# Attention on one core: seven product units in each bank, and q and k rounded to fp16 by GpSimd's loading queue from the second batch on

## The chip, the cores and the metric

The kernel runs on one core of a Trainium2 chip. The metric is the device time of one execution in microseconds; lower is better. Most executions of a kernel agree within a per cent. The "granted clock" below is the share of its full clock that TensorE was given, as the profile records it. The span that a profile gives is shorter than the time by about 1.8 us, in the kernel before.

## The reference

It is plain softmax attention: 8 batches of 8 heads, 512 positions, 64 dimensions, all fp32.

```python
def reference(q, k, v):                       # each (8, 8, 512, 64) fp32
    scale = 1.0 / np.sqrt(q.shape[-1])
    scores = np.einsum('bhqd,bhkd->bhqk', q, k) * scale
    scores = scores - scores.max(axis=-1, keepdims=True)
    attn = np.exp(scores)
    attn = attn / attn.sum(axis=-1, keepdims=True)
    return np.einsum('bhqk,bhkd->bhqd', attn, v).astype(np.float32)
```

## The kernel before

The 64 heads are handled as 32 pairs. For each pair, q, k and v come in as fp32 from the SyncE queue, 256 KB each, and GpSimd rounds them to fp16. For q and k it also lays the two heads side by side, so that one transpose of 128 columns serves both.

```python
def load(g, names):                            # one pair: 128 x (2 heads x 4 x 64) fp32
    ...
        nc.sync.dma_start(out=t[:, :, :, :], in_=source(src, g))

def cast_qk(g):
    t = qpool.tile([P, 2, NI, P], FP16, tag="qkp", name=f"qkp_{g}")
    for n, name in ((1, "k"), (0, "q")):
        nc.gpsimd.tensor_copy(
            out=t[:, n].rearrange("p i (h d) -> p h i d", h=2),
            in_=raw[g][name][:, :, :, :],
        )

def transposes(g, n):                          # n = 0: q, n = 1: k; tps is one PSUM bank
    ...
    for i in range(NI):
        nc.tensor.transpose(tps[g][:, n, i, :], qkp[g][:, n, i, :], ident)
```

VectorE copies the bank of a pair's transposes out. Scores are matmuls of 64x512; two of them make a group of 128x1024, which ScalarE turns into exponentials (`pt`). Products of `pt` with v (and a column of ones) fill one bank for each head: four units of 65 columns. VectorE divides by the sum and stores.

```python
def normalise(g, h):
    o = os.pop((g, h))                         # 128 x 4 x 65
    nc.vector.reciprocal(out=rc[:, :, :], in_=o[:, :, D : D + 1])
    nc.vector.tensor_tensor(out=ob[:, h], in0=o[:, :, 0:D],
                            in1=rc[:, :, :].broadcast_to([P, NI, D]), op=AluOp.mult)
    if g == LAST:
        nc.sync.dma_start(out=source(out, g)[:, h], in_=ob[:, h])
    elif not first:                            # the pair's second head
        nc.sync.dma_start(out=source(out, g), in_=ob[:, :, :, :])
```

Four of the 129 groups are given to VectorE instead of ScalarE: a "raise" and ten passes of integer and polynomial work. A small planner in Python (`Plan`), with estimated durations, fixes the order of all instructions when the kernel is built. Each engine then works through its list in order, so an instruction that isn't ready holds all that stand behind it on its engine.

The softmax here doesn't subtract the row's maximum and nothing guards it: scores larger than these inputs give would overflow.

Of the kernel before, what the change touches and what calls it, by code (L numbers as in the profile page):

```python
# [14 lines left out]

class Plan:

# [7 lines left out]
    T_UNIT, V_UNIT = 224, 130  # L25
    TO_ACT, TO_DVE, TO_PE = 275, 210, 60
    COPY, NORM = 700, 640
    RAISE, PASS, LATE = 1210, 690, 300
    STEP = 5

    def __init__(self, groups, pairs, first, share):
        self.groups, self.pairs, self.share = groups, pairs, share
        self.pe, self.act, self.dve = 6700, 7820, 6800
        self.m, self.tiled = first, True
        self.done = {}
        self.exps = {}
        for m in range(first):
            self.done[m] = self.exps[m] = 6000 + m * 904 + self.EXP_DONE
        self.tq = {0: 6800}
        self.next_t = 1  # L40
        self.bank = [6000, 6800]
        self.jobs = 0
        self.job = None
        self.todo = [(g, h) for g in range(pairs) for h in range(2)]
        self.member = {}
        for m, grp in enumerate(groups):
            for b in grp:
                self.member[b] = m
        self.evacs = []
        self.raises = []  # L50
        self.poly = []
        self.steps = []

# [9 lines left out]
    def blocks_done(self, g, h, chunks=range(4)):  # L63
        return max(self.exps.get(self.member[(g, c, h)], 1e9) for c in chunks)

    def free(self, m):
        g = self.groups[m][0][0]
        return max(self.done.get(m - 3, 1e9) if m >= 3 else 0, self.tq.get(g, 1e9))

    def issue(self, t):  # L70
        m, grp = self.m, self.groups[self.m]
        g = grp[0][0]
        heads = [b[2] for b in grp]
        slots = 1 if len(set(heads)) == 2 else len(grp)
        on_dve = (
            self.share
            and not self.poly
            and not self.raises
            and 2 <= g < self.pairs - 7
            and m % 4 == 1  # L80
        )
        self.note(t, "scores", m, on_dve)
        t += (0 if self.tiled else self.INTO) + self.SLOT * slots
        self.tiled = True
        if on_dve:
            self.raises.append((t + self.TO_DVE, m))
        else:
            n = len(grp)
            begin = max(self.act, t + self.TO_ACT)
            self.act = begin + self.EXP * n // 2 + self.EXP_FIXED  # L90
            self.done[m] = self.exps[m] = self.act + self.EXP_DONE - self.EXP - self.EXP_FIXED
        self.m += 1
        self.pe = t

    def pick(self, t):
        cur = self.groups[min(self.m, len(self.groups) - 1)][0][0]
        n = self.jobs
        if t + 40 < self.bank[n % 2]:
            return None
        g = self.next_t  # L100
        can_t = g < self.pairs and g <= cur + 2 and t >= self.ready_kq(g)
        if can_t and g <= cur + 1:
            return ("t", g)
        for g2, h in self.todo[:8]:
            last = (g2, h) == (self.pairs - 1, 1)
            chunks = (0,) if last else range(4)
            if t >= self.blocks_done(g2, h, chunks) and t >= self.ready_v(g2):
                return ("v", g2, h)
        return ("t", g) if can_t else None

    def unit_ready(self):
        what, part = self.job[0], self.job[1]
        if what[0] == "v" and what[1:] == (self.pairs - 1, 1):
            return self.blocks_done(what[1], what[2], (part,))
        return 0

    def fill(self, t):
        if self.job is None:
            what = self.pick(t)
            if what is None:  # L120
                return False
            self.job = [what, 0, self.jobs]
            self.jobs += 1
            self.bank[self.job[2] % 2] = 1e9
            if what[0] == "t":
                self.next_t += 1
            else:
                self.todo.remove(what[1:])
        if t < self.unit_ready():
            return False  # L130
        what, part, n = self.job
        cost = (self.T_UNIT if what[0] == "t" else self.V_UNIT) + (self.OUT_OF if self.tiled else 0)
        self.tiled = False
        self.note(t, "unit", what, part)
        self.pe = t + cost
        self.job[1] += 1
        if self.job[1] == (2 if what[0] == "t" else 4):
            self.evacs.append((self.pe + self.TO_DVE, what, n))
            self.job = None
        return True  # L140

    def step_pe(self, t):
        if self.m < len(self.groups):
            now = t >= self.free(self.m)
            more = self.m + 1 < len(self.groups) and t >= self.free(self.m + 1)
            slack = self.act - t
            if now and (more or slack < 1100):
                return self.issue(t)
            soon = self.free(self.m)
            if not now and slack < 1300 and soon < t + 150:  # L150
                return
        else:
            now = False
        if not self.fill(t) and now:
            self.issue(t)

    def step_dve(self, t):
        if self.raises and self.raises[0][0] <= t:
            ready, m = self.raises.pop(0)
            self.note(t, "raise", m)  # L160
            self.dve = t + self.RAISE
            self.done[m] = self.dve + self.TO_PE
            self.poly = [(m, s) for s in range(10)]
            return
        if self.evacs and self.evacs[0][0] <= t:
            ready, what, n = self.evacs.pop(0)
            self.note(t, "evac", what)
            self.dve = t + (self.COPY if what[0] == "t" else self.NORM)
            self.bank[n % 2] = self.dve + self.TO_PE
            if what[0] == "t":  # L170
                self.tq[what[1]] = self.dve + self.TO_PE
            return
        coming = [x[0] for x in self.raises + self.evacs]
        if self.poly and min(coming, default=1e9) > t + self.PASS - self.LATE:
            m, s = self.poly.pop(0)
            self.note(t, "pass", m, s)
            self.dve = t + self.PASS
            if s == 9:
                self.exps[m] = self.dve + self.TO_PE

    def run(self):
        t = min(self.pe, self.dve)
        while self.m < len(self.groups) or self.todo or self.job or self.evacs or self.poly:
# [8 lines left out]

# [3 lines left out]
def kernel(  # L196
# [27 lines left out]
    M = len(groups)  # L224
# [3 lines left out]
    qpool = ctx.enter_context(tc.tile_pool(name="qk16", bufs=3))  # L228
    tpool = ctx.enter_context(tc.tile_pool(name="tqk", bufs=4))
    ppool = ctx.enter_context(tc.tile_pool(name="pt", bufs=36))  # L230
# [6 lines left out]
    NV = 12  # L237
    vps = [cpool.tile([P, 2, NI, D + 1], FP16, name=f"vp{n}") for n in range(NV)]
# [9 lines left out]
    obs = {}  # L248
# [6 lines left out]
    def load_tile(g, name):  # L255
        t = lpool.tile([P, 2, NI, D], FP32, tag=f"{name}32", name=f"{name}32_{g}")
# [10 lines left out]

    def cast_v(g):
        nc.gpsimd.tensor_copy(out=vps[g % NV][:, :, :, 0:D], in_=raw[g]["v"][:, :, :, :])  # L269

    def cast_qk(g):
        if g >= NP:
            return
# [7 lines left out]

    def transposes(g, n):
# [3 lines left out]
        for i in range(NI):  # L286
            nc.tensor.transpose(tps[g][:, n, i, :], qkp[g][:, n, i, :], ident)  # L287
# [6 lines left out]
    def scores(m, on_dve=False):  # L294
# [41 lines left out]
    def pass_(m, s):  # L336
# [12 lines left out]
        if s == 1:  # L349
# [10 lines left out]
        n, x = divmod(s - 2, 2)  # L360
        mant = r["m"][:, x, :].bitcast(FP32)
        nc.vector.scalar_tensor_tensor(  # L362
            out=r["pt"][:, x, :] if n == 3 else r["y"][:, x, :],
            in0=mant if n == 0 else r["y"][:, x, :],
            scalar=QUARTIC[n],
            in1=r["e"][:, x, :].bitcast(FP32) if n == 3 else mant,
# [4 lines left out]
    def normalise(g, h):  # L371
        o = os.pop((g, h))
        first = g not in obs
        if first:
            obs[g] = opool.tile([P, 2, NI, D], FP32, tag="ob", name=f"ob_{g}")
        ob = obs[g]
        rc = opool.tile([P, NI, 1], FP32, tag="rc", name=f"rc_{g}_{h}")
        nc.vector.reciprocal(out=rc[:, :, :], in_=o[:, :, D : D + 1])  # L378
        nc.vector.tensor_tensor(  # L379
            out=ob[:, h],  # L380
            in0=o[:, :, 0:D],
            in1=rc[:, :, :].broadcast_to([P, NI, D]),
            op=AluOp.mult,
        )
        if g == LAST:
            nc.sync.dma_start(out=source(out, g)[:, h], in_=ob[:, h])
        elif not first:
            nc.sync.dma_start(out=source(out, g), in_=ob[:, :, :, :])

    def values(g, h, part):  # L390


        last = g == LAST and h == 1
# [149 lines left out]
```

## Time and profile before

| what | value |
|---|---|
| time, median of 3 | 125.89 us (125.25 to 126.57) |
| span of the profiled execution | 126.3 us; that execution took 128.07 us and counts as slow |
| ScalarE, TensorE, VectorE, GpSimd busy | 115.7, 113.3, 93.5, 66.9 us |
| groups on ScalarE, on VectorE | 125, 4 |

The transfer engines are busy for four fifths of the time, and early in the kernel they are full. (The share adds up the packets' times over 16 engines; it passes 1 where packets of one engine overlap.) This is the view by stretch, with the engines' busy time, the granted clock, the DMA share and GB/s at its end:

```profile
8.00:16.00 8.00, 7.77 (x72) 4.43 (x70) 3.12 (x7) 6.71 (x8) 6.21 (x11) 1.00 1.07 373
```

### The profile page before, as it was taken

The numbers are of one execution on the slowest core, as the hardware profiler recorded it, in microseconds if no ns is written. First come the engines' busy times: TensorE is split into PE (matmuls) and PEld (weight loads), VectorE is DVE, ScalarE is ACT, GpSimd is POOL, SyncE is SP. The second block draws the span as 40 slices with busy tenths as digits, with TensorE's granted clock in tenths as the row PEclk, the third lists the DMA queues.
The fourth block names the chain that finished last, engine by engine and source line by source line (L and its number), as shares of the span: only waits on it lengthen the run. The fifth ranks groups of instructions, "written<-read, shape, count | busy, mean of one in ns | idle before, by whom it ended". The sixth has DMA issues, their size and how long they took to land.

```text
span 126.3 us, 4005 instructions
## 1 busy us (share of the span) xinstructions
PE 113.3 (90%) x1550; PEld 67.9 (54%) x1550; DVE 93.5 (74%) x211; ACT 115.7 (92%) x127; POOL 66.9 (53%) x117
## 2 busy tenths in 40 slices
PE   6999999888899889888998899889988989899870
PEld 2437555555566555555665555555645555665450
DVE  0514598998896898786779999868799997565340
ACT  4086899999999999999999999999999999999970
POOL 6558897976471475786049736451688551000000
PEclk9999999999999999999999999999999999999999
DMA  3999999999887799998999777999998951243203
GB/s 119 309 331 372 381 378 384 383 365 298 279 308 211 190 368 378 369 309 271 294 341 283 261 248 260 309 353 335 353 285 282 274 177 55 88 143 108 87 28 140
DMA packets 34883, 33.82 MB, mean 268 GB/s; under 512 B 2096, under 2 KB 34864, under 8 KB 34864
## 3 DMA queue, kind: packets, MB, share of 16 engines
q1 hardware_dynamic: 34576, 33.30, 80.3%
q10 hardware_dynamic: 288, 0.26, 0.6%
q8 instruction: 12, 0.20, 0.6%
q14 instruction: 7, 0.06, 0.2%
HBM read 25.17 MB, written 8.39 MB: 266 GB/s over the span
## 4 chain that ended last, share of the span: by engine, by line
ACT 41%; PE 38%; issue 15%; DMA 2%; DVE 1%; POOL 0%; ACTq 0%
ACT pt L313 41%; PE st L302 16%; PE o L399 14%; PE tp L287 6%; DMA k<-in_k_dram 2%; PE tp_k L437 1%; PE tp_q L437 1%; DVE ob L379 1%; DVE rc L378 0%; POOL qkp L428 0%; ACTq L313 0%
## 5 line engine op out<-in xcount | busy, mean ns | idle before, releaser
L313 ACT ACTIVATE pt<-st 128x1024 f16<-128x1024 f32 (+1 forms) x125 | 114.2, 1339 | 4.5 <-PE st L302 4.5
L399 PE MATMUL o<-vp,pt 128*128 128x65 f16 x1024 | 52.0, 196 | 6.5 <-ACT pt L313 5.7
L399 PEld LDWEIGHTS <-pt 128*128 128x128 f16 x1024 | 39.0, 99 | 29.1 <-issue 17.5
L302 PE MATMUL st<-tqk 64*128 64x512 f16 x256 | 52.4, 396 | 1.1 <-ACT pt L313 0.5
L276 POOL CAST qkp<-k 128x512 f16<-128x512 f32 x31 | 22.2, 716 | 28.2 <-DMA k<-in_k_dram 15.5
L379 DVE TENSOR_TENSOR ob<-o,rc 128x256 f32<-128x256 f32 x64 | 27.2, 425 | 2.2
L290 DVE COPY tqk<-tp 128x1024 f16<-128x1024 f16 x31 | 21.2, 684 | 7.0 <-PE tp L287 7.0
L269 POOL CAST vp<-v 128x512 f16<-128x512 f32 x32 | 22.5, 702 | 5.7 <-DMA v<-in_v_dram 5.1
L378 DVE RECIPROCAL rc<-o 128x4 f32<-128x4 f32 x64 | 11.5, 179 | 15.7 <-PE o L399 14.8
L276 POOL CAST qkp<-q 128x512 f16<-128x512 f32 x31 | 21.3, 686 | 2.4 <-DMA q<-in_q_dram 2.1
L302 PEld LDWEIGHTS <-tqk 64*128 64x128 f16 x256 | 13.0, 94 | 15.9 <-issue 8.9
L287 PE MATMUL tp<-ident,qkp 128*128 128x128 f16 x248 | 20.1, 225 | 0.6 <-DVE ob L379 0.4
L287 PEld LDWEIGHTS <-qkp 128*128 128x128 f16 x248 | 14.9, 100 | 5.6 <-POOL qkp L276 2.9
L362 DVE SCALAR_TENSOR_TENSOR y<-y,m 128x512 f32<-128x512 f32 x16 | 12.5, 779 | 0.0
L362 DVE SCALAR_TENSOR_TENSOR y<-m 128x512 f32<-128x512 f32 x8 | 7.1, 890 | 0.0
L362 DVE SCALAR_TENSOR_TENSOR pt<-y,e 128x512 f16<-128x512 f32 x8 | 6.1, 764 | 0.0
L327 DVE TENSOR_SCALAR z<-st 128x1024 uint32<-128x1024 f32 x4 | 4.9, 1220 | 0.1
L351 DVE TENSOR_SCALAR e<-z 128x1024 uint32<-128x1024 uint32 x4 | 3.9, 969 | 0.0
L486 PE MATMUL warm<-zeros 128*128 128x512 f16 x6 | 2.7, 630 | 1.2 <-DVE zeros L480 1.2
L340 DVE TENSOR_SCALAR m<-z 128x1024 uint32<-128x1024 uint32 x4 | 3.5, 870 | 0.0
L427 ACT ACT_TABLE_LOAD x1 | 1.3, 1283 | 1.7 <-PEq L527 1.7
L437 PEld LDWEIGHTS <-qkp 128*128 128x128 f16 x16 | 1.5, 135 | 1.8 <-issue 1.0
(20 smaller groups left out, 9.7 us busy)
## 6 DMA issues: line engine op xcount, KB each, us to landing
v<-in_v_dram SPq DMA_DIRECT2D x32, 256.0 KB, 5.2
k<-in_k_dram SPq DMA_DIRECT2D x31, 256.0 KB, 4.7
q<-in_q_dram SPq DMA_DIRECT2D x31, 256.0 KB, 5.0
out_dram<-ob SPq DMA_DIRECT2D x31, 256.0 KB, 3.8
k<-in_k_dram ACTq DMA_DIRECT2D x2, 128.0 KB, 3.0
q<-in_q_dram SPq DMA_DIRECT2D x2, 128.0 KB, 2.8
out_dram<-ob SPq DMA_DIRECT2D x2, 128.0 KB, 1.8
```

Source lines behind the costliest of these rows:

```text
L269: nc.gpsimd.tensor_copy(out=vps[g % NV][:, :, :, 0:D], in_=raw[g]["v"][:, :, :, :])
L276: nc.gpsimd.tensor_copy(out=t[:, n].rearrange("p i (h d) -> p h i d", h=2), in_=raw[g][name][:, :, :, :],)
L287: nc.tensor.transpose(tps[g][:, n, i, :], qkp[g][:, n, i, :], ident)
L290: nc.vector.tensor_copy(out=tqk[g][:, :, :], in_=tps.pop(g).rearrange("p n i c -> p n (i c)"))
L302: nc.tensor.matmul(st[:, x, :], tqk[g][po : po + 64, 1, c * P : (c + 1) * P], tqk[g][po : po + 64, 0, :], start=True, stop=True,)
L313: nc.scalar.activation(out=pt[:, 0:size, :], in_=st[:, 0:size, :], func=EXP, scale=scale)
L327: nc.vector.tensor_scalar(out=r["z"][:, :, :], in0=r["st"][:, :, :], scalar1=scale * 1.4426950408889634 * 2.0**23, scalar2=(127 + SHIFT) * ...
L362: nc.vector.scalar_tensor_tensor(out=r["pt"][:, x, :] if n == 3 else r["y"][:, x, :], in0=mant if n == 0 else r["y"][:, x, :], scalar=QUAR ...
L378: nc.vector.reciprocal(out=rc[:, :, :], in_=o[:, :, D : D + 1])
L379: nc.vector.tensor_tensor(out=ob[:, h], in0=o[:, :, 0:D], in1=rc[:, :, :].broadcast_to([P, NI, D]), op=AluOp.mult,)
L399: nc.tensor.matmul(o[:, qc, :], blocks[(g, c, h)][:, qc * P : (qc + 1) * P], vps[g % NV][:, h, c, :], start=(c == 0 and (qc == 0 or not la ...
L437: nc.tensor.transpose(dst, halves[h][:, n, i, :], ident)
```

## The change

The change has two halves. In the first, the packing, product units are packed seven to a bank, so that VectorE divides 448 elements at a time instead of 256, stores go out head by head from a ring, and VectorE's polynomial works on whole groups. The time that this frees on VectorE goes into two more groups of exponentials. The second half takes the rounding of q and k off GpSimd: from the second batch on, a transfer of a whole batch rounds on its way. Its data then lies head by head, so each head is transposed by itself, 64 columns at a time, into its half of the bank. Only pairs 0 to 3 (the first batch) still go the old way.

```diff
+    def load_batch(b):
+        t = bpool.tile([P, 2, H, NI, D], FP16, tag="qk16", name=f"qk16_{b}")
+        for n, src in ((1, k), (0, q)):
+            nc.gpsimd.dma_start(
+                out=t[:, n], in_=src[b].rearrange("h (p i) d -> p h i d", i=NI)
+            )
+        for x in range(ppb):                       # ppb = 4 pairs in a batch
+            qkp[b * ppb + x] = t[:, :, 2 * x : 2 * x + 2]
...
     def cast_qk(g):
-        if g >= NP:
+        if g >= ppb:
             return
...
+    def feed(g):
+        if g % ppb == 1:
+            load_batch(g // ppb + 2)
+        load(g + 5, "v")
+        cast_qk(g + 3)
+        cast_v(g + 2)
...
         for i in range(NI):
-            nc.tensor.transpose(tps[g][:, n, i, :], qkp[g][:, n, i, :], ident)
+            if g < ppb:
+                nc.tensor.transpose(tps[g][:, n, i, :], qkp[g][:, n, i, :], ident)
+                continue
+            for h in range(2):
+                nc.tensor.transpose(
+                    tps[g][64 * h : 64 * h + 64, n, i, :], qkp[g][:, n, h, i, :], ident
+                )
...
+    def normalise(u, n):                           # n = 7 units, 4 at the very end
+        o = os[u // 7]
+        nc.vector.reciprocal(out=rc[:, 0:n], in_=o[:, 0:n, D : D + 1])
+        nc.vector.tensor_tensor(out=ring[:, u % NU : u % NU + n, :], ...)
+        while heads and heads[0][2] + NI <= u + n:
+            g, h, first = heads.pop(0)
+            nc.sync.dma_start(
+                out=source(out, g)[:, h], in_=ring[:, first % NU : first % NU + NI, :]
+            )
...
         cast_qk(2)
         cast_v(1)
         feed(0)
+        load_batch(1)
```

The planner's rules change with it (which groups VectorE takes, how far it looks for products). By order of instructions there are 123 groups on ScalarE and 6 on VectorE.

## The prediction

> **What bounds the kernel now.** I read the page's busy table first, then the costliest groups, then ScalarE's own timeline, then the waits of TensorE, and last the start of TensorE, GpSimd and the load queue.
>
> ```profile
> PE 113.3 (90%) x1550; PEld 67.9 (54%) x1550; DVE 93.5 (74%) x211; ACT 115.7 (92%) x127; POOL 66.9 (53%) x117
> ...
> L313 ACT ACTIVATE pt<-st 128x1024 f16<-128x1024 f32 (+1 forms) x125 | 114.2, 1339 | 4.5 <-PE st L302 4.5
> ...
> L379 DVE TENSOR_TENSOR ob<-o,rc 128x256 f32<-128x256 f32 x64 | 27.2, 425 | 2.2
> L290 DVE COPY tqk<-tp 128x1024 f16<-128x1024 f16 x31 | 21.2, 684 | 7.0 <-PE tp L287 7.0
> ```
>
> Two engines are near 90%. The 4.5 us of idle time ahead of the exponentials lies wholly at the start, as ScalarE's timeline shows:
>
> ```profile
> 6.45 1.02 ACT L313 ACTIVATE pt<-st 128x1024 f16<-128x1024 f32 x1 [2.69 <-PE st L302]
> ...
> 14.04 108.33 ACT L313 ACTIVATE pt<-st 128x1024 f16<-128x1024 f32 x119 [0.33 <-PE st L302]
> ```
>
> From 14.04 us to 122.37 us ScalarE never stops: 119 instructions, of which the last two are half size, so about 108.33 / 118 = 0.92 us for each full one. The remaining 3.9 us of the 126.3 us span are the last products, divisions and stores. The kernel is bound by ScalarE, and every exponential group that VectorE takes is worth 0.92 us. The second question is how much room TensorE has. Its waits between 14 and 118 us:
>
> ```profile
> PEld L399 <- issue: 16.6, 73, 0.3
> PEld L399 <- ACT pt L313: 8.0, 19, 0.5
> ```
>
> "Issue" at a change between scores and other work is lost array time. Only about 8 us (the 19 weight loads that wait for ScalarE, which overlap the waits of their products) is slack. So TensorE could take some 8 us more before it became the bound.
>
> **What the Trainium skill says.** "DMA: Bandwidth & Descriptors", section "SWDGE vs HWDGE vs iDMA": a transfer that changes type can only be issued from GpSimd, whose cores write the descriptors; its "Latency and other measured facts" gives about 1 us to the first byte on that path. The kernel before has no such transfer, so its trace cannot confirm this. "TensorEngine Tiling (Array Packing)", sections "Key Properties" and "Restrictions": a change of tiling mode drains the array, and column tiling turns the fast weight load off. "TensorE: Matmul & The Clock Gate", section "LDWEIGHTS", gives columns / 1.2 ns for a slow load, 53 ns for 64 columns. The trace agrees on the drains (the issue waits of 0.23 us at changes between scores and products); it has no column tiles. "SBUF — State Buffer", section "Who interferes with whom": a VectorE instruction with two SBUF inputs contends with GpSimd reads. The trace agrees: casts on GpSimd take 0.62 us, but 1.07 us beside the polynomial.
>
> **The change part by part.**
>
> *Exponentials.* By order of instructions the changed program has 123 exponential instructions on ScalarE (two of them half size) and 6 groups on VectorE, where there were 125 and 4. Gain: 2 x 0.92 = 1.8 us, on the path.
>
> *VectorE.* Normalising: 64 pairs of 179 + 425 = 38.7 us become 36 of seven units and one of four. The fixed part of the multiply is 425 - 256/0.96 = 158 ns by my estimate at one element per cycle of a clock of 0.96 GHz (the slope that the 1,024-element raise of 1220 ns also allows), so 448 elements take 625 ns: 36 x (0.18 + 0.63) + 0.6 = 29.8 us, or 9 us less. Two more groups: 6 x 1.22 for the raise, 6 x (0.87 + 0.97) for the integer passes and 24 whole passes of about 1.25 us (half ones take 0.76 to 0.89) come to 48.3 us, against 38.0. So VectorE goes from 93.5 to about 95 us. It stays off the bound, but single waits are longer, because a pass is now twice as long.
>
> *GpSimd.* 56 casts of 0.7 us = 39 us leave; 14 loads of 1 MiB, cast on the way, come. GpSimd was not the bound, so nothing of this shows by itself. It also gains against VectorE's lock.
>
> *Loads.* Queue 1 moved 34,576 packets in 80.3% of 16 engines' 126.3 us, 46.9 ns each. If a packet of 1 KB read and 512 B written costs the same, the share stays near 80%. Early on the queues are full (373 GB/s from 8 to 16 us, DMA share 1.07), so there loads decide.
>
> *TensorE.* For 28 pairs, 8 transposes of 128 columns become 16 of 64, two heads side by side in column tiles. If the two tiles run together and loads are hidden, nothing changes (8 take 0.61 us). If the 16 weight loads of 53 ns follow one another, a pair takes 0.85 us, plus a drain of 0.1 us at each of the 15 direct changes from transposes to products: at most 28 x 0.24 + 1.5 = 8 us, all of the slack. Changes to and from scores hardly differ in number (99 each way before, 94 after). I take half, 4 us, hidden but for 0.3 us.
>
> *The second batch's first arrival.* This is the cost I believe in most. The load of batch 1 stands on GpSimd behind all casts of the first pairs:
>
> ```profile
> 11.79 0.62 POOL L276 CAST qkp<-q 128x512 f16<-128x512 f32 x1
> 12.44 0.62 POOL L269 CAST vp<-v 128x512 f16<-128x512 f32 x1
> ```
>
> Those end at 13.1 us and do not change. The load needs no wait, yet starts only then: 2.1 MB at 373 GB/s is 5.6 us, and I add some 2 us for first byte and completion (the very first load, 128 KB with three like it, took 2.88 us, of which about 1.4 is data) and 0.7 us for a load of v between. It lands at about 21.5 us. TensorE asks for it far sooner. In the new order the transposes of pair 4 follow the scores of group 11; before, their first half stood in the same place:
>
> ```profile
> 16.96 0.39 PE L302 MATMUL st<-tqk 64*128 64x512 f16 x2
> 17.29 0.40 PE L287 MATMUL tp<-ident,qkp 128*128 128x128 f16 x4
> ```
>
> TensorE works in order, and the first half wants q, which is the later of the two transfers. It would stand from 17.3 to 21.5 us. ScalarE then has groups 10 and 11 to do (groups 9 and 11 would end near 18.6 us in either order), and the next scores come about 1.0 us after the landing (transposes 0.6, one unit of products 0.15, scores 0.3), with 0.3 us to ScalarE: 22.8 us. ScalarE stands for 4.2 us. Nothing later gives this back, since it ran without a gap anyway. Later batches are issued over 20 us ahead and are hidden.
>
> *Sum.* 125.9 - 1.8 (two groups) + 4.2 (first arrival) + 0.3 (TensorE) - 0.1 (banks shared at the start) = 128.5 us.
>
> **Rivals.**
> 1. The batch arrives in time, or TensorE's lead covers it. For it: the queue is otherwise empty at 13 us, as the loads of q and k for pairs 4 and 5 are gone, and ScalarE has about 1.6 us of work in store. Against: 5.6 us of data alone end at 18.7 us. This makes 124 to 125.5 us.
> 2. Casting transfers run slower than plain ones. Nothing in the trace speaks to it. At twice the time per packet, 14,336 packets x 94 ns / 16 = 84 us and the other 20,240 x 46.9 / 16 = 59 us exceed the span: DMA bound, about 145 us; at 1.5 times they need 122 us and the first arrival slips by 3 us more: 131 to 134 us.
> 3. TensorE becomes the bound: the weight loads in column tiles are serial and the drains come on top. The slack of 8 us speaks against more than 1 to 3 us; 129 to 131 us together with the stall.
> 4. Writing 4 x 1,024 descriptors holds GpSimd so long that the cast of v for pair 3, which stands behind them, is late (wanted at about 23 us). That adds 1 to 4 us more.
>
> **Range and chances.** The gain is sure and small (1.8 us, 1.4%); it cannot by itself pass 2%. The stall is likely, with a size from 1 to 8 us; rivals 2 to 4 only add. Faster by 2% needs under 123.4 us, so no stall and 0.7 us from elsewhere: 0.07. Slower by 2% starts at 128.4 us, just where my sum lies: 0.48. Within 2%: 0.45. Range 124.2 to 135 us.
>
> **What would show it.** In the changed profile: 123 exponentials (two of them half size) on ScalarE; TensorE's first wait for the fp16 tile of batch 1, 3 to 5 us long near 17 us, and an idle piece on ScalarE near 19 us of about 4 us; afterwards ScalarE without gaps; the time of 16 transposes between 0.6 and 0.9 us; VectorE near 95 us busy; DMA share near 80%. I am wrong if the batch lands by 18 us, if ScalarE has many small gaps later (TensorE or VectorE the bound), or if the DMA share is near full throughout.

## More of the kernel before

Besides the lines that the prediction shows, three more of the page matter later. The first is the share of the 16 transfer engines that the loading and storing queue took (packets, MB, share). The others are groups of instructions: what GpSimd spent on rounding k, and what TensorE spent on transposes (busy us, mean ns of one, then the idle time ahead of them and what ended it).

```profile
q1 hardware_dynamic: 34576, 33.30, 80.3%
...
L276 POOL CAST qkp<-k 128x512 f16<-128x512 f32 x31 | 22.2, 716 | 28.2 <-DMA k<-in_k_dram 15.5
...
L287 PE MATMUL tp<-ident,qkp 128*128 128x128 f16 x248 | 20.1, 225 | 0.6 <-DVE ob L379 0.4
```

GpSimd's casts of q and k are 22.2 + 21.3 = 43.5 us of work on an engine that isn't the bound.

## The result, and the profile after

The changed kernel takes 137.03 us (median of 4 runs, 136.68 to 137.77), against 126.23 us for the kernel before in the same rounds (125.25 to 127.06). Executions over 1.5% slower than the fastest of the same kernel are left out of the means. Ratios in this document are the mean time of one kernel's fast runs over that of the other's of the same rounds, so not quite the ratio of the medians. Here the ratio is 1.087, with a 95% interval of 1.077 to 1.096. The change is slower by nearly 9%; 128.5 us was predicted, in a range of 124.2 to 135 us.

These lines of the page of the changed kernel answer to those shown of before:

```profile
PE 112.6 (83%) x1774; PEld 69.2 (51%) x1774; DVE 95.3 (71%) x155; ACT 114.1 (85%) x125; POOL 42.7 (32%) x75
...
q1 hardware_dynamic: 19840, 18.62, 43.8%
q0 software_dynamic: 14560, 7.34, 42.7%
...
L368 ACT ACTIVATE pt<-st 128x1024 f16<-128x1024 f32 (+1 forms) x123 | 112.6, 1242 | 12.3 <-PE st L357 12.3
...
L345 DVE COPY tqk<-tp 128x1024 f16<-128x1024 f16 x31 | 21.3, 687 | 14.8 <-PE tp L340 9.2
...
L340 PE MATMUL tp<-ident,qk 128*64 128x128 f16 x448 | 18.5, 225 | 7.2 <-DMA qk<-in_q_dram 7.2
L430 DVE TENSOR_TENSOR ring<-o,rc 128x448 f32<-128x448 f32 (+1 forms) x37 | 22.9, 619 | 1.6 <-DMA out_dram<-ring 0.3
```

Nothing became much costlier as work: TensorE has 112.6 us (113.3 before), ScalarE 114.1 (115.7), GpSimd 42.7 (66.9). What grew is ScalarE's idle time before exponentials, from 4.5 us to 12.3. ScalarE's timeline (start, duration, then in brackets the idle time before it) shows where it lies:

```profile
13.98 4.69 ACT L368 ACTIVATE pt<-st 128x1024 f16<-128x1024 f32 x5 [0.43 <-PE st L357]
26.11 1.02 ACT L368 ACTIVATE pt<-st 128x1024 f16<-128x1024 f32 x1 [7.45 <-PE st L357]
27.42 101.03 ACT L368 ACTIVATE pt<-st 128x1024 f16<-128x1024 f32 x111 [0.29 <-PE st L357]
```

ScalarE runs dry at 18.67 us, stands for 7.45 us, and then works from 27.42 us to 128.45 without a gap. Its 111 instructions there, two of them half size, make 101.03 / 110 = 0.92 us each, as before. So the steady pace is the same, and nearly all of the idle time that was added is one event. TensorE's waits, over the whole span, name what it was:

```profile
PEld L453 <- issue: 14.8, 60, 0.4
...
PEld L340 <- DMA qk<-in_q_dram: 7.5, 1, 7.5
```

There is one wait of 7.5 us for q of the second batch, and no other for a casting load. The timeline of GpSimd and TensorE around it:

```profile
12.55 1.01 POOL L302 DMA_DIRECT2D qk<-in_k_dram  x1
...
16.52 0.39 PE L357 MATMUL st<-tqk 64*128 64x512 f16 x2
...
24.13 1.06 PE L340 MATMUL tp<-ident,qk 128*64 128x128 f16 x16 [7.22 <-DMA qk<-in_q_dram]
...
28.18 0.64 PE L340 MATMUL tp<-ident,qk 128*64 128x128 f16 x16
```

The loads of k and q are issued by GpSimd from 12.55 us on; TensorE has nothing else it may do from 16.9 us, and starts on q at 24.13. The 16 transposes there take 1.06 us, and 0.64 us at the next pair, since TensorE came out of the wait at half its clock, as the view by stretch shows (columns as above: PE, PEld, DVE, ACT, POOL, then clock, DMA share, GB/s written):

```profile
10.00:12.50 2.50, 2.50 (x28) 1.57 (x26) 0.69 (x1) 1.55 (x2) 2.30 (x4) 1.00 1.09 383
...
14.00:16.00 2.00, 1.94 (x24) 1.09 (x22) 1.74 (x3) 2.00 (x3) 2.00 (x3) 1.00 0.79 76
...
18.00:20.00 2.00, 0.00 (x0) 0.00 (x0) 0.00 (x0) 0.67 (x1) 2.00 (x4) 1.00 1.39 200
...
22.00:24.00 2.00, 0.00 (x0) 0.00 (x0) 0.00 (x0) 0.00 (x0) 0.62 (x1) 0.50 1.31 244
24.00:26.00 2.00, 1.87 (x22) 1.17 (x23) 0.76 (x2) 0.00 (x0) 0.62 (x1) 0.50 1.46 197
```

Read the last two numbers of each row. Until 12.5 us plain loads keep the transfer engines full (383 GB/s). From 14 to 16 us the share is 0.79 (0.80 from 12.5 to 14): the plain loads have thinned out and the casting load is only starting. From 18 to 24 us the casting loads share the engines with loads of v and stores. In the last row nothing but casting packets moved, at 197 GB/s written. As these write half of what they read, that is some 400 GB/s read, so the casting queue isn't slow once it runs.

The trace's packets show how the load passed. The first packet of the casting queue starts at 14.29 us, 1.74 us after the issue. Its 2,048th data packet, which completes the count for k and q of one batch, starts at 22.10; that is 262 a microsecond, with 430 packets of v and stores beside it in that time. Each of the 16 transfer engines then writes one small packet when it is done with q: 15 of them do so between 21.48 and 22.65 us, the last at 23.76. TensorE starts 0.37 us after that one. GpSimd had issued the third batch's load right behind this one, from 14.42 us on; no run takes it away, so whether it delayed the last engine isn't shown.

At the other end of the kernel there is a second, smaller loss. These are the last products, the stores and the last division, first of the kernel before, then of the changed one:

```profile
122.12 0.65 PE L399 MATMUL o<-vp,pt 128*128 128x65 f16 x16 [0.32 <-DVE rc L378]
122.55 1.28 SPq L386 DMA_DIRECT2D out_dram<-ob  x2
...
123.03 0.42 DVE L379 TENSOR_TENSOR ob<-o,rc 128x256 f32<-128x256 f32 x1
```

```profile
119.87 12.14 SPq L438 DMA_DIRECT2D out_dram<-ring  x12
...
128.95 0.65 PE L453 MATMUL o<-vp,pt 128*128 128x65 f16 x16 [0.15 <-DVE ring L430]
...
129.86 0.43 DVE L430 TENSOR_TENSOR ring<-o,rc 128x256 f32<-128x256 f32 x1
```

From ScalarE's last exponential to the end of the span it was 126.3 - 122.4 = 3.9 us; it is now 134.9 - 128.45 = 6.4. Of the added 2.5 us, 0.75 come from products that end 1.15 us after ScalarE instead of 0.40. Most of the rest is the queue of stores: the last store was issued at 131.63 us, 1.3 us after its division had ended at 130.29, because SyncE was still issuing the one before it. In the kernel before, the last store was issued at 123.48 us, 0.03 us after its division.

### The profile page after: what moved, and what is told of

Its sections match the earlier page's. It is cut to its first block, busy times and chain, and to the rows that moved or that the text cites. A ratio compares the mean times of both kernels' runs of the same rounds, so it can differ in the third digit from the quotient of the medians.

```text
span 134.9 us, 4255 instructions
## 1 busy us (share of the span) xinstructions
PE 112.6 (83%) x1774; PEld 69.2 (51%) x1774; DVE 95.3 (71%) x155; ACT 114.1 (85%) x125; POOL 42.7 (32%) x75
## 3 DMA queue, kind: packets, MB, share of 16 engines
q1 hardware_dynamic: 19840, 18.62, 43.8%
q0 software_dynamic: 14560, 7.34, 42.7%
## 4 chain that ended last, share of the span: by engine, by line
ACT 39%; PE 25%; DMA 19%; issue 9%; DVE 2%; POOL 1%; SPq 1%; ACTq 0%
ACT pt L368 39%; PE o L453 11%; PE st L357 10%; DMA qk<-in_q_dram 8%; DMA v<-in_v_dram 4%; PE tp L340 4%; DMA out_dram<-ring 4%; DMA k<-in_k_dram 4%; DVE ring L430 2%; POOL qk L302 1%; SPq L467 1%; DVE rc L429 1%; POOL vp L311 0%; ACTq L368 0%
## 5 line engine op out<-in xcount | busy, mean ns | idle before, releaser
L368 ACT ACTIVATE pt<-st 128x1024 f16<-128x1024 f32 (+1 forms) x123 | 112.6, 1242 | 12.3 <-PE st L357 12.3
L340 PE MATMUL tp<-ident,qk 128*64 128x128 f16 x448 | 18.5, 225 | 7.2 <-DMA qk<-in_q_dram 7.2
L430 DVE TENSOR_TENSOR ring<-o,rc 128x448 f32<-128x448 f32 (+1 forms) x37 | 22.9, 619 | 1.6 <-DMA out_dram<-ring 0.3
L340 PEld LDWEIGHTS <-qk 128*64 128x64 f16 x448 | 13.7, 111 | 13.5 <-DMA qk<-in_q_dram 7.5
L429 DVE RECIPROCAL rc<-o 128x7 f32<-128x7 f32 (+1 forms) x37 | 7.5, 202 | 13.4 <-PE o L453 13.2
L417 DVE SCALAR_TENSOR_TENSOR y<-y,m 128x1024 f32<-128x1024 f32 x12 | 14.6, 1216 | 0.0
L417 DVE SCALAR_TENSOR_TENSOR y<-m 128x1024 f32<-128x1024 f32 x6 | 7.7, 1284 | 0.0
L417 DVE SCALAR_TENSOR_TENSOR pt<-y,e 128x1024 f16<-128x1024 f32 x6 | 7.7, 1275 | 0.0
L382 DVE TENSOR_SCALAR z<-st 128x1024 uint32<-128x1024 f32 x6 | 7.3, 1220 | 0.4 <-PE st L357 0.4
L302 POOL DMA_DIRECT2D qk<-in_k_dram x7 | 6.3, 899 | 0.0
L337 PEld LDWEIGHTS <-qkp 128*128 128x128 f16 x24 | 2.0, 127 | 2.3 <-POOL vp L311 0.8
L337 PE MATMUL tp<-ident,qkp 128*128 128x128 f16 x24 | 2.9, 281 | 0.0
```

Of the source, the lines that this page charges most:

```text
L302: nc.gpsimd.dma_start(out=t[:, n], in_=src[b].rearrange("h (p i) d -> p h i d", i=NI))
L340: nc.tensor.transpose(tps[g][64 * h : 64 * h + 64, n, i, :], qkp[g][:, n, h, i, :], ident)
L368: nc.scalar.activation(out=pt[:, 0:size, :], in_=st[:, 0:size, :], func=EXP, scale=scale)
L382: nc.vector.tensor_scalar(out=r["z"][:, :, :], in0=r["st"][:, :, :], scalar1=scale * 1.4426950408889634 * 2.0**23, scalar2=(127 + SHIFT) * ...
L417: nc.vector.scalar_tensor_tensor(out=r["pt"][:, :, :] if n == 3 else r["y"][:, :, :], in0=mant if n == 0 else r["y"][:, :, :], scalar=QUAR ...
L429: nc.vector.reciprocal(out=rc[:, 0:n], in_=o[:, 0:n, D : D + 1])
```

## The experiments

The two readings to be told apart were these. By the first, the loss is the arrival of the second batch alone, and the packing and the half transposes cost nothing. By the second, part of it comes from the denser use of VectorE, from the half transposes, or from a casting queue that is slower throughout. Within the first reading it was open whether an earlier issue would help, or whether the transfer engines are so full at the start that the load only trades places with others. All nine results were correct. The kernel before ran beside them in each set: 125.95, 125.77 and 125.47 us in the medians.

**The kernel before once more.** No edit.

> The kernel before, unchanged, for a profile in the fast state (the profile on file was taken in an execution of 128.07 us, 1.5% above the others). All theories: about 126 us, a span near 124.2 us (the time less the 1.8 us that both profiled executions lay outside their span). It shows which part of the span was 2 us longer in the old profile: the start before ScalarE's steady stretch, the steady stretch of 0.918 us a step, or the 3.9 us after ScalarE's last instruction.

It took 126.13 us with a span of 124.3; its span is that of the fast runs. The profile of before that the prediction worked from was a slow execution (128.07 us). The difference lies at the start. Here are TensorE's scores of the first groups and ScalarE's timeline in this run:

```profile
6.68 1.61 PE L302 MATMUL st<-tqk 64*128 64x512 f16 x6
```

```profile
6.25 114.19 ACT L313 ACTIVATE pt<-st 128x1024 f16<-128x1024 f32 x125 [2.69 <-PE st L302]
```

In the slow execution the same six scores took longer:

```profile
6.88 2.45 PE L302 MATMUL st<-tqk 64*128 64x512 f16 x6
```

So in a fast start ScalarE never pauses after its first exponential, whereas the slow one lost 4.5 - 2.7 = 1.8 us there. The views give a granted clock of 1.00 for both, but only because the trace has no clock entry for the first microseconds, which they count as full. The first entry, of the full clock, starts at 13.76 us in the slow execution and at 6.66 us in this one. In all eleven traces the work follows that entry: the four scores that are due near 9 to 11 us take 1.03 us where it is still to come (first entry at 13.8 to 14.0 us: the old profile of before, the changed kernel, the half transposes) and 0.60 us where it has come (4.3 to 6.7 us, the other eight). So a slow start is a full clock that is granted late; why it comes late in some executions isn't shown. This matters for a stall at 18 us: a run with a fast start arrives there with 1.8 us less work left, and waits 1.8 us longer for the same landing.

**The packing alone.** All pairs take the old loads, casts and full transposes; packing and plan stay as in the changed kernel. (The buffers for q and k go back from four to six, here and in the next two runs.)

```diff
     def cast_qk(g):
-        if g >= ppb:
+        if g >= NP:
...
-        if g % ppb == 1:
-            load_batch(g // ppb + 2)
+        if g + 6 < NP:
+            load(g + 6, "kq")
...
-        load_batch(1)
```

> The changed program's packing and plan, with all q and k loaded in fp32 by SyncE's queue and cast on GpSimd, and full 128-column transposes, as before. Theory A (the loss is the wait for the first casting load, and the tail costs 2.6 us): the stall of 7.9 us goes, 137.0 - 7.9 = 129 us. Theory B (packing and plan are the 1.8 us gain that I predicted and cost nothing at the end; all the loss is in the loads): 124.4 us. Theory C (the plan's longer VectorE passes and shared banks starve ScalarE): above 130 us, with gaps of ScalarE in mid-kernel.

It took 125.42 us (125.08 to 126.28), ratio 0.998 (0.988 to 1.007): the same as before. ScalarE's timeline in it:

```profile
5.73 112.00 ACT L367 ACTIVATE pt<-st 128x1024 f16<-128x1024 f32 x123 [2.10 <-PE st L356]
```

ScalarE ends at 117.73 us, 2.7 us sooner than in the run of the kernel before above (6.25 + 114.19 = 120.44), without a pause. The end of the kernel then takes 123.7 - 117.73 = 6.0 us instead of 124.3 - 120.44 = 3.9. Of these 2.7 us, 0.5 are an earlier start (5.73 against 6.25 us), in an execution whose first clock entry is at 4.37 us instead of 6.66, and 2.2 are the exponentials (112.00 against 114.19 us). So the packing earns 2.2 us and gives back 2.1 in the last products and stores, where the last store is again issued 1.3 us after its division. In sum it loses nothing: the loss of 11 us comes from the other half of the change.

**The half transposes alone.** As the last, but from pair 4 on with the 64-column transposes, taken from the same packed tile.

```diff
             for h in range(2):
                 nc.tensor.transpose(
-                    tps[g][64 * h : 64 * h + 64, n, i, :], qkp[g][:, n, h, i, :], ident
+                    tps[g][64 * h : 64 * h + 64, n, i, :], qkp[g][:, n, i, 64 * h : 64 * h + 64], ident
                 )
```

> As the run with the packing only, but with the 64-column transposes of each head into its half of the bank from pair 4 on; loads and casts as before. Theory A (two column tiles run side by side, as the 0.57 us for 16 in the changed profile says): equal to the packing only within 0.5%. My prediction's term (serial weight loads): 16 take 0.85 us, TensorE has 4 to 8 us more to do, and the time is up to 3 us longer.

It took 125.69 us, with one slow run of four at 128.14; the ratio of the fast runs is 0.998 (0.990 to 1.006), that of the packing alone to three digits. The group of transposes on the page, first in the packing alone, then here:

```profile
L336 PE MATMUL tp<-ident,qkp 128*128 128x128 f16 x248 | 19.5, 220 | 0.2 <-DVE ring L429 0.2
```

```profile
L339 PE MATMUL tp<-ident,qkp 128*64 128x128 f16 x448 | 18.0, 222 | 0.2 <-DVE ring L429 0.2
```

The 28 pairs x 16 = 448 half transposes are busy for 18.0 us; 224 of the 248 full ones, which they replace, make 19.5 x 224 / 248 = 17.6 us. (The profile here is of the slow run, but its late clock had come at 14.0 us, and the first half transposes start at 16.88.) So two halves cost what one full transpose did, and the time shows no loss.

**Casting loads from the third batch on.** The second batch also goes the old way, so the first casting load is the third batch's.

```diff
-        if g >= ppb:
+        if g >= 2 * ppb:
...
+        if g + 6 < 2 * ppb:
+            load(g + 6, "kq")
...
-        load_batch(1)
```

> The changed kernel, but the second batch (pairs 4 to 7) also by the old loads and casts; casting loads from the third batch on, issued at the same place in the plan as before. Theory A (only the first casting load comes too late, since it stands behind the casts and is wanted 4.5 us after its issue): no wait of TensorE for a casting load, ScalarE without a stall, and 129 us, within 1% of the packing only. Theory B (casting loads are slow enough, 60 ns a packet against 46, to be late wherever they start): a stall of several us moves to the first pair of the third batch, near 30 us, and the time stays above 133 us.

It took 126.98 us (126.03 to 127.47), ratio 1.008 (0.999 to 1.016); against the fast runs of the packing alone it is 126.86 / 125.55, or 1% more. So 24 of the 28 pairs can be loaded by the casting queue at the cost of about 1.3 us, little more than the spread of the runs, and the second batch carries nearly all of the loss. Part of that 1.3 us is seen in the timeline: the third batch, too, was not quite in time. ScalarE pauses there:

```profile
31.35 88.20 ACT L370 ACTIVATE pt<-st 128x1024 f16<-128x1024 f32 x97 [0.81 <-PE st L359]
```

The load had been issued at 12.07 us, but the first packet of the casting queue started only at 16.02 and its 2,048th data packet at 29.21, while the plain loads of the second batch used the same engines. Beside other loads, this one took some 17 us from the issue of q (13.07 us) to TensorE's start on it (30.34 us).

**The same load issued earlier.** The two transfers of the second batch go to GpSimd ahead of the casts of pairs 2 and 3.

```diff
         cast_qk(1)
         cast_v(0)
+        load_batch(1)
         cast_qk(2)
         cast_v(1)
         feed(0)
-        load_batch(1)
```

> The changed kernel, but GpSimd issues the first casting load right after its cast of v for pair 0, some 4.5 us earlier (8.0 instead of 12.55 us). Theory A (the place in GpSimd's order is the cause): it lands 4.5 us sooner, near 19.6 us, the stall shrinks from 7.6 to about 3 us, and the time is 132.5 us. Theory B (what counts is how much the transfer engines must move before then; they are full until 12.3 us and idle only from 12.3 to 14.3 us): it lands at most 2 us sooner, the loads of pairs 2 and 3 come later because the two queues share the engines, and the time is 135 us or more.

It took 135.00 us (133.87 to 135.68), ratio 1.074 (1.066 to 1.081). The issue moved from 12.55 to 9.21 us, 3.3 us, and the restart of ScalarE only from 26.11 to 25.20:

```profile
25.20 1.02 ACT L368 ACTIVATE pt<-st 128x1024 f16<-128x1024 f32 x1 [6.96 <-PE st L357]
```

The first casting packet started at 12.20 us, 3.0 us after its issue, when the plain loads of the first batch had thinned out (382 and 376 GB/s from 8 to 12 us, then 238). The 2,048th data packet started at 20.71. Nearly three quarters of the head start were lost in this execution, beside the loads that still used the engines, and GpSimd's 1.9 us of issuing delayed the casts of pairs 2 and 3, which cost ScalarE a pause of 1.20 us at 13.55 us. The profile is of the slowest of the four runs; by the medians the head start was worth 2.0 us (137.03 - 135.00) of a loss of 11. So the place of the issue is a minor part of the loss, as theory B has it. That the larger part is what must be moved by then is argued here; the pieces below test it.

**Stores of the end on two queues.** Once all scores are issued, the stores of odd heads go to ScalarE's queue (the lines that count the scores are left out).

```diff
-            nc.sync.dma_start(
+            queue = nc.scalar if issued[0] == len(groups) and h == 1 else nc.sync
+            queue.dma_start(
```

> The changed kernel; once all scores are issued, the stores of every second head go to ScalarE's queue instead of SyncE's. In the changed profile the last store is issued 1.3 us after the last division, behind others on one queue; before, at once. Theory A (the issue of single-head stores on one queue is half of the longer end): 1.0 to 1.3 us less, 135.8 us. Theory B (the end is bound by the products and divisions, or by the landing): no change within 0.3 us.

It took 136.55 us (136.25 to 137.24), ratio 1.088 (1.083 to 1.093), so not told from the changed kernel. In the profiled run the end after ScalarE shrank to 133.3 - 128.3 = 5.0 us, but that run's time (136.34 us) shows little of it, and the spans of its three other runs are 134.3 to 135.5; for the end alone this run is inconclusive. It is telling about the stall, because it had the fast start:

```profile
25.96 1.02 ACT L369 ACTIVATE pt<-st 128x1024 f16<-128x1024 f32 x1 [9.96 <-PE st L358]
```

ScalarE ran dry at 16.00 us (18.67 in the changed kernel's profile) and restarted at 25.96 (26.11). The stall grew by 2.5 us and the restart hardly moved. The arrival of the batch sets the time of all that follows, and a better start is swallowed by it.

**The first casting load in pieces.** The second batch comes in eight transfers, k and q pair by pair, at the same place (the loop that is replaced is left out).

```diff
+        cuts = [(2 * x, 2 * x + 2) for x in range(ppb)] if b == 1 else [(0, H)]
+        for h0, h1 in cuts:
+            for n, src in ((1, k), (0, q)):
+                nc.gpsimd.dma_start(
+                    out=t[:, n, h0:h1],
+                    in_=src[b, h0:h1].rearrange("h (p i) d -> p h i d", i=NI),
+                )
```

> The changed kernel, but the first casting load is issued pair by pair (eight transfers of 128 KB written instead of two of 512 KB), in the same place. Theory A (TensorE waits for q of all eight heads, although pair 4 wants a quarter of it): q and k of pair 4 land near 18.0 us (14.3 us first packet, 512 packets, and 2 us), the stall of ScalarE shrinks from 7.6 to about 1.5 us, and the time is 131 us less the start that no longer hides behind the stall: 127.5 to 131 us. Theory B (the casting queue starts too late and is too slow for any pair): pairs 5 to 7 stall as well, and the time stays above 134 us. It also shows whether GpSimd's 0.88 us for a casting load goes with its descriptors (0.22 us then) or is fixed.

It took 132.18 us (130.95 to 133.86, the last one slow), ratio of the fast runs 1.057 (1.048 to 1.066). About half of the loss (137.03 - 132.18 = 4.9 us) was in the size of the piece that TensorE had to wait for. TensorE's first transposes of the batch, and ScalarE's restart:

```profile
17.02 1.06 PE L343 MATMUL tp<-ident,qk 128*64 128x128 f16 x16 [2.19 <-DMA qk<-in_q_dram]
```

```profile
18.99 1.02 ACT L371 ACTIVATE pt<-st 128x1024 f16<-128x1024 f32 x1 [2.41 <-PE st L360]
```

The first pair's 512 data packets were all started by 16.01 us and TensorE began at 17.02 instead of 24.13. But the whole batch was no sooner through: its 2,048th data packet started at 22.76 us. GpSimd needed 0.72 to 0.83 us for these transfers of 256 packets, against 0.88 us for one of 1,024, so pieces multiply its work. Later pauses of ScalarE (0.29, 0.16 and 0.75 us) follow. The last, up to 61.11 us, has the clock behind it: the trace has a granted clock of 0.50 from 57.87 to 61.28 us, and 16 half transposes took 1.07 us there; why it fell is open. The stall of 2.41 us was near theory A's 1.5, but the median missed both theories. Its fastest run, 130.95 us, is still over 5 us above the packing alone.

**The packing with stores on two queues.** The packing alone, with the edit of the end.

> The packing only (loads and casts as before) with the last stores on two queues. Theory A: the packing's own gain of 2.7 us on ScalarE's side was paid back by 2.0 us at the end, of which 1.3 us is the issue of stores: 125.4 - 1.2 = 124.2 us, about 1.4% faster than the kernel before. Theory B: no change, 125.4 us.

Its fast runs took 124.54 and 124.55 us (theory A: 124.2), two slow ones 126.99 and 127.16; the median of all four is 125.77. The ratio of the fast runs is 0.991 (0.986 to 0.996). The end after ScalarE is 122.8 - 117.67 = 5.1 us, 0.9 less than with the packing alone, and the last store is issued 0.04 us after its division. By its two fast runs this is the best version, ahead of the kernel before by 0.9%, which is small.

**The first pair ahead.** q and k of pair 4 alone are issued early (as in the earlier issue above), pairs 5 to 7 in one transfer of k and one of q at the old place (`load_batch` now takes a range of heads; that edit is left out).

```diff
         cast_v(0)
+        load_batch(1, 0, 2)
         cast_qk(2)
         cast_v(1)
         feed(0)
-        load_batch(1)
+        load_batch(1, 2, H)
```

> The changed kernel, but the first casting load is cut in two: q and k of pair 4 alone are issued right after the cast of v for pair 0 (256 KB written, near 8 to 9 us), those of pairs 5 to 7 where the whole stood. Theory A (the loss is only that the whole batch must land before pair 4 can go): pair 4 lands by 15 us, before it is wanted at 16 to 17 us; pair 5 is wanted near 20 us and its load lands near 22 us, so a stall of 1 to 2 us is left: 128 to 130 us, less than the 132.2 us of the pieces. Theory B (the early plain loads lose to the casting queue as much as is won): the loads of pairs 2 and 3 come later by some 2 us and stall ScalarE before pair 4; the time is no better than 132 us.

It took 132.82 us (132.17 to 133.61), ratio 1.056 (1.052 to 1.060). TensorE's transposes of pair 4, and of pair 5:

```profile
15.92 0.64 PE L344 MATMUL tp<-ident,qk 128*64 128x128 f16 x16 [0.71 <-DMA qk<-in_q_dram]
...
23.92 1.07 PE L344 MATMUL tp<-ident,qk 128*64 128x128 f16 x16 [5.22 <-DMA qk<-in_q_dram]
```

The wait for pair 4 has gone, and one of 5.22 us for pair 5 has come, at nearly the same time (23.92 us) at which the changed kernel had waited for pair 4. ScalarE pauses for 5.19 us there. Giving one pair a start moves the stall by one pair's worth of work, about 4 us, and no more; theory A's 128 to 130 us was missed. The other three pairs come in one transfer, whose last byte is again what is waited for.

## Why the prediction was wrong

**The mechanism was right, and so was its place.** "The second batch's first arrival" was named as the cost to believe in most. ScalarE ran dry at 18.67 us (18.6 predicted), on TensorE's wait for q of the second batch, after the scores that were named, and afterwards it ran without gaps. The experiments show that it is this one load: without it (the packing alone, the half transposes alone, casting from the third batch) the ratios are 0.998, 0.998 and 1.008, with it 1.074 to 1.088, and with only a part of it to wait for at first 1.056 and 1.057.

**The term that failed is the size of the stall: 4.2 us predicted, 9.6 measured** (12.3 us of idle time of ScalarE before exponentials, against 2.7 in an execution of the kernel before with a fast start; the 9.6 are 7.45 of the stall, 0.29 just after it, and 1.86 in three pauses ahead of it). The error has four parts.

| part | predicted | measured | error |
|---|---|---|---|
| landing: TensorE starts on the batch | 21.5 us | 24.13 us | +2.6 |
| from there to ScalarE's restart | 1.3 us | 1.98 us | +0.7 |
| a second pause just after it | none | 0.29 us | +0.3 |
| pauses of the slow start | none counted | 1.86 us | +1.9 |

These sum to 5.5, and 4.2 + 5.5 = 9.7. The landing breaks down further. I had 13.1 us for the issue, 5.6 of data, 0.7 for v and "some 2 us for first byte and completion". Measured were the issue at 12.55 us (0.55 sooner), 1.74 us to the first packet, 7.81 us from the first to the 2,048th data packet (1.5 more than 6.3), and 2.03 us from there to TensorE's start. The fixed parts are thus 3.8 us instead of 2, because a first byte on this path alone took 1.7, and because "landed" means that the slowest of 16 engines is done, here 1.1 us after the 15th. That the data took longer than the full rate gives fits with what the views show: the engines were not full from 14 to 16 us, and v and stores were moved alongside. No run parts the two. I had taken the rate of a queue in steady flow for a single load that has just been issued.

The restart was slower because TensorE's granted clock fell to 0.50 during the wait (from 20.77 to 27.60 us in the trace): transposes 1.06 instead of 0.64 us, two scores 0.61 instead of 0.39. I had used durations at full clock.

The fourth error is one of method. I read times of events from an execution that was 1.8 us behind, and added the stall so found to the median of executions that were not. The changed kernel's own profile had the slow start, so its early pauses of 1.86 us count against a base that had none. With a fast start ScalarE runs out sooner, and the stall is longer instead; the run with the stores on two queues shows 9.96 us and the same restart.

**A term that was missing: the end, +2.5 us.** The prediction carried over the last 3.9 us of the kernel before unchanged. The diff had said otherwise: in place of one store for each pair there is one for each head, 64 instead of 33, and a bank of seven units waits for more than one head. The packing alone shows the same (+2.1 us), so this is the packing's own cost. That the issuing of stores makes much of it is supported by the packing with two store queues (0.9 us less); it was not shown for the changed kernel itself.

**Two groups fewer: right.** ScalarE's exponentials go from 114.19 us (in the run of before with the fast start) to 112.55, a gain of 1.6 us where 1.8 was predicted (2.2 in the packing alone, where they run without a break).

**The sum.** 125.9 - 1.6 + 9.6 + 2.5 = 136.4 us; the profiled run took 136.68, the median 137.03. The 0.6 us between the sum and the median are less than the spread of the four runs (1.1), and I have no cause for them.

**TensorE: the cautious 0.3 us was not needed.** I expected 16 transposes to take 0.6 to 0.9 us. They take 0.64 us in a row at full clock (8 full ones 0.62), and the half transposes alone cost nothing: neither the serial weight loads nor the drains of 0.1 us, for which I had named no trace, show in its time.

**VectorE and GpSimd: right.** VectorE is busy for 95.3 us, with about 95 predicted. (The slope of 0.96 elements a nanosecond comes out of the prediction's own two figures, 1,024 - 256 elements in 1220 - 425 ns; 36 divisions of 448 elements and one of 256 average 619 ns, where 625 was estimated for 448.) The batch loads cost GpSimd 0.88 us each, and no cast of v was late for it in the changed kernel before the stall.

**DMA share: off.** 43.8 + 42.7 = 86.5%, where near 80% was predicted, since a casting packet's record is longer than a plain one's: 42.7% x 16 x 134.9 us / 14,560 = 63 ns, against 43.8% x 16 x 134.9 / 19,840 = 48. It doesn't bind: ScalarE has no pause after 27.4 us.

**The rivals.** "The batch arrives in time" fell. "Casting transfers run slower than plain ones" fell as a rate (some 400 GB/s read against 383 plain), though what it would have made of the time, 131 to 134 us, came nearer than my own sum; it would have been right for another reason. "TensorE becomes the bound" fell with the half transposes alone. "Writing descriptors holds GpSimd" fell for the changed kernel, but showed itself in the earlier issue, where it cost a pause of 1.20 us.

**Why the change doesn't pay here.** It takes 24 us off GpSimd (66.9 to 42.7), an engine that is off the path that sets the end. What it asks in exchange is that a first load of 2 MB, all of which must have landed, arrives about 4 us after it is issued, beside other loads.

## What to carry to other kernels

A load that is made larger, or moved to another queue, should be judged first by its first arrival: count from the issue to the first packet, all of the bytes ahead of the last one at the rate of engines that are shared, and the slowest engine's completion, and compare with the moment at which its first reader wants it; its steady rate alone doesn't tell this. When adding a stall to a base time, take both from executions in the same state, because a stall that ends at a fixed arrival swallows whatever was gained ahead of it. And taking work off an engine that is not the bound earned nothing here, so such a change should cost nothing on the path, which is best tested by undoing its halves one at a time, as the packing alone did here.

## What the Trainium skill lacked or had wrong

- "DMA: Bandwidth & Descriptors", section "Latency and other measured facts", gives about 1 us to the first byte of a transfer issued by GpSimd. In the changed kernel it was 1.74 us from the start of the issue to the first packet, and 3.0 and 4.0 us when plain loads filled the engines (the earlier issue, and the casting loads from the third batch on). It has no rate for transfers that change type: here 197 GB/s written from twice as much read, so not below the 383 GB/s of the plain loads. It has no figure for what such a transfer costs GpSimd: 0.88 us for 1,024 packets, and still 0.72 to 0.83 us for 256.
- "TensorE: Matmul & The Clock Gate", section "LDWEIGHTS", gives the time of one slow weight load, from which I had estimated 16 x 53 ns = 0.85 us for a pair. Neither it nor the tiling page has a figure for transposes in two column tiles of 64 side by side, though the tiling page does have tiles work in parallel: here 16 half transposes took 0.64 us in a row, 8 full ones 0.62, and the kernel with half transposes had the same ratio to before (0.998) as the one without.
- That the full clock comes only after some work, and at different times in different executions, is in "TensorE: Matmul & The Clock Gate", section "What's actually happening". It has no start as late as those seen here: the first entry of the full clock lay at 13.8 to 14.0 us in three of eleven traces (4.3 to 6.7 in the others), the same six scores took 2.45 instead of 1.61 us, and the execution ended 2 us later. What makes it come so late stays open.
